# Multi-query attention on one core: fp16 transposes, fewer borrowed score buffers, and a new order of scores and weighted sums

## Chip, cores, metric

One NeuronCore of a Trainium2 chip. The metric is the device time of one execution in microseconds (us). All durations below are in us unless marked ns.

## What the kernel must compute

```python
# q: (8, 1024, 16, 64) float32; k, v: (8, 1024, 64) float32, shared by the 16 heads of a batch
scores  = q @ k^T / sqrt(64)
weights = softmax(scores)            # over the keys
out     = weights @ v                # (8, 1024, 16, 64) float32
```

Of the kernel before, what the change touches and what calls it, by code (L numbers as in the profile page):

```python
# [16 lines left out]
def kernel(  # L17
# [19 lines left out]
    KPS = NKT // SPG  # L37
    NP = (B * H) // 2
    HP = H // 2
    HHALF = H // 2  # L40
    scale = 1.0 / math.sqrt(D)

    consts = ctx.enter_context(tc.tile_pool(name="consts", bufs=1))
    qnatp = ctx.enter_context(tc.tile_pool(name="qnatp", bufs=2))
    kvp = ctx.enter_context(tc.tile_pool(name="kvp", bufs=2))
    qtp = ctx.enter_context(tc.tile_pool(name="qtp", bufs=3))
    wtp = ctx.enter_context(tc.tile_pool(name="wtp", bufs=2 * NKT + 2))
    otsp = ctx.enter_context(tc.tile_pool(name="otsp", bufs=4))
    recp = ctx.enter_context(tc.tile_pool(name="recp", bufs=4))
    osbp = ctx.enter_context(tc.tile_pool(name="osbp", bufs=3))  # L50

    scp = ctx.enter_context(tc.tile_pool(name="scp", bufs=3, space=bass.MemoryType.PSUM))
# [1 line left out]

    ident = consts.tile([P, P], FP32)
    make_identity(nc, ident)

    k2t: dict = {}
    vpr: dict = {}
    qnat: dict = {}  # L60
    qt_tiles: dict = {}
    wt_tiles: dict = {}
    ot_psum: dict = {}
# [3 lines left out]
    def emit_batch_load(b):  # L67
        if b >= B or b in k2t:
            return
        knat = kvp.tile([P, NKT, D], FP32, tag="knat", name=f"knat{b}")  # L70
        vnat = kvp.tile([P, NKT, D], FP32, tag="vnat", name=f"vnat{b}")
        nc.sync.dma_start(out=knat, in_=k[b].rearrange("(c p) d -> p c d", p=P))
        nc.sync.dma_start(out=vnat, in_=v[b].rearrange("(c p) d -> p c d", p=P))  # L73
        slabs = []
        for half in range(2):
            qn = qnatp.tile(
                [P, NKT, HHALF * D], FP32, tag="qnat", name=f"qnat{b}_{half}"
            )
            nc.sync.dma_start(
                out=qn,  # L80
                in_=q[b, :, half * HHALF : (half + 1) * HHALF, :].rearrange(
                    "(c p) h d -> p c (h d)", p=P
                ),
            )
            slabs.append(qn)
        qnat[b] = slabs
        kk = kvp.tile([P, S], FP16, tag="k2t", name=f"k2t{b}")
        n_stage = max(1, S // QCH)
        per = S // n_stage
        for cs in range(n_stage):  # L90
            kps = scp.tile([P, 2, QCH], FP32, tag="sc", name=f"kps{b}_{cs}")
            for jj in range(per // P):
                src = knat[:, cs * (per // P) + jj, :]
                nc.tensor.matmul(  # L94
                    kps[0:64, 0, jj * P : (jj + 1) * P],
                    src,
                    ident,
                    start=True,
                    stop=True,
                    tile_position=(0, 0),  # L100
                )
                nc.tensor.matmul(  # L102
                    kps[64:128, 0, jj * P : (jj + 1) * P],
                    src,
                    ident,
                    start=True,
                    stop=True,
                    tile_position=(0, 64),
                )
            nc.vector.tensor_copy(  # L110
                out=kk[:, cs * per : (cs + 1) * per], in_=kps[:, 0, 0:per]
            )
        k2t[b] = kk
        vp = kvp.tile([P, NKT, 66], FP16, tag="vpr", name=f"vpr{b}")
        nc.vector.tensor_copy(out=vp[:, :, 0:64], in_=vnat)  # L115
        nc.vector.memset(vp[:, :, 64:65], 1.0)
        vpr[b] = vp

    def emit_qtrans(p, part):
        if p >= NP:  # L120
            return
        b, hp = divmod(p, HP)
        emit_batch_load(b)
        if p not in qt_tiles:
            qt_tiles[p] = qtp.tile([P, S], FP16, tag="qt", name=f"qt{p}")
        qt = qt_tiles[p]
        nchunk = NQB // 2
        st = scp.tile([P, 2, QCH], FP32, tag="sc", name=f"qst{p}_{part}")
        half, hloc = divmod(2 * hp, HHALF)
        for c in range(nchunk):  # L130
            sc_idx = part * nchunk + c
            src = qnat[b][half][:, sc_idx, hloc * D : (hloc + 2) * D]
            nc.tensor.matmul(  # L133
                st[:, c // 4, (c % 4) * P : (c % 4) * P + P],
                src,
                ident,
                start=True,
                stop=True,
            )
        width = nchunk * P  # L140
        assert width <= QCH
        nc.vector.tensor_copy(  # L142
            out=qt[:, part * width : (part + 1) * width], in_=st[:, 0, 0:width]
        )

    def emit_qk(p, j, c):
        b = p // HP
        sc = scp.tile([P, 2, QCH], FP32, tag="sc", name=f"sc{p}_{j}_{c}")
        kk = k2t[b]
        qt = qt_tiles[p]  # L150
        nc.tensor.matmul(  # L151
            sc[:, 0, :],
            kk[0:64, j * P : (j + 1) * P],
            qt[0:64, c * QCH : (c + 1) * QCH],
            start=True,
            stop=True,
            tile_position=(0, 0),
        )
        nc.tensor.matmul(  # L159
            sc[:, 1, :],  # L160
            kk[64:128, j * P : (j + 1) * P],
            qt[64:128, c * QCH : (c + 1) * QCH],
            start=True,
            stop=True,
            tile_position=(64, 0),
        )
        key = (p, j)
        if key not in wt_tiles:
            wt_tiles[key] = wtp.tile([P, 2, S], FP16, tag="wt", name=f"wt{p}_{j}")
        wt = wt_tiles[key]  # L170
        nc.scalar.activation(  # L171
            out=wt[:, :, c * QCH : (c + 1) * QCH], in_=sc, func=EXP, scale=scale
        )
# [28 lines left out]

    def emit_finish(p, hh):
        b, hp = divmod(p, HP)
        ots = ots_tiles.pop((p, hh))
        if p not in osb_tiles:
            osb_tiles[p] = osbp.tile([P, NQB, 2 * D], FP32, tag="osb", name=f"osb{p}")
        osb = osb_tiles[p]
        for gq in range((NQB + 3) // 4):
            nblk = min(4, NQB - gq * 4)  # L210
            tr = scp.tile([P, 2, QCH], FP32, tag="sc", name=f"tr{p}_{hh}_{gq}")
            for i in range(nblk):
                qb = gq * 4 + i
                nc.tensor.matmul(  # L214
                    tr[:, 0, i * P : i * P + 65],
                    ots[0:65, qb * P : (qb + 1) * P],
                    ident[0:65, 0:65],
                    is_transpose=True,
                    start=True,
                    stop=True,  # L220
                )
            trv = tr[:, 0, :].rearrange("p (blk x) -> p blk x", x=P)[:, 0:nblk, :]
            rec = recp.tile([P, 4], FP32, tag="rec", name=f"rec{p}_{hh}_{gq}")
            nc.vector.reciprocal(out=rec[:, 0:nblk], in_=trv[:, :, 64:65])  # L224
            nc.vector.tensor_tensor(  # L225
                out=osb[:, gq * 4 : gq * 4 + nblk, hh * D : (hh + 1) * D],
                in0=trv[:, :, 0:64],
                in1=rec[:, 0:nblk].unsqueeze(2).broadcast_to([P, nblk, D]),
                op=mybir.AluOpType.mult,
            )  # L230
        if hh == 1:
            nc.sync.dma_start(
                out=out[b, :, 2 * hp : 2 * hp + 2, :].rearrange(
                    "(qb p) h d -> p qb (h d)", p=P
                ),
                in_=osb_tiles.pop(p),
            )

    emit_batch_load(0)
    emit_qtrans(0, 0)  # L240
    emit_qtrans(0, 1)
    stepA = (NGRP - 1) * SPG
    for w in range(NP + 2):
        pQK = w
        pAV = w - 1
        for j in range(NKT):
            if j == 0 and (w - 2, 1) in ots_tiles:
                emit_finish(w - 2, 1)
            if 0 <= pAV < NP:
                g = j // SPG  # L250
                sub = j % SPG
                emit_av(pAV, g, list(range(sub * KPS, (sub + 1) * KPS)))
            if pQK < NP:
                for c in range(NQC):
                    emit_qk(pQK, j, c)
            if j == 2:
                emit_qtrans(pQK + 1, 0)
            elif j == 3:
                emit_qtrans(pQK + 1, 1)
            if j == 5 and (pQK + 2) < NP and (pQK + 2) % HP == 0:  # L260
                emit_batch_load((pQK + 2) // HP)
            if j == stepA and (pAV, 0) in ots_tiles:
                emit_finish(pAV, 0)


# [28 lines left out]
```

## The kernel before

It works on 64 head pairs (8 batches of 8 pairs). In one round `w` of the main loop the scores and exponentials of pair `w` are made beside the weighted sums ("AV") of pair `w-1`. A round has eight rows `j`, one for each block of 128 keys. A row makes two score tiles of 128 keys x (2 heads x 512 queries), each turned into weights by one exponential on ScalarE. An added column of ones in v gives the softmax denominator.

```python
scp = ctx.enter_context(tc.tile_pool(name="scp", bufs=3, space=PSUM))   # score buffers, 2 banks each
otp = ctx.enter_context(tc.tile_pool(name="otp", bufs=2, space=PSUM))   # AV accumulators
...
def emit_qtrans(p, part):            # half of a q transpose: 4 blocks, fp32, one score buffer
    st = scp.tile([P, 2, QCH], FP32, tag="sc")
    for c in range(4):
        nc.tensor.matmul(st[:, 0, c*P:(c+1)*P], qnat_block_fp32, ident_fp32, start=True, stop=True)
    nc.vector.tensor_copy(out=qt[:, half], in_=st[:, 0, :])             # to fp16
...
def emit_finish(p, hh):              # output of one head: 2 x 4 transposes, two score buffers
    for gq in range(2):
        tr = scp.tile([P, 2, QCH], FP32, tag="sc")
        # 4 transposes of 65x128, then reciprocal and multiply on VectorE
...
for w in range(NP + 2):              # pQK = w, pAV = w - 1
    for j in range(8):
        if j == 0: emit_finish(w - 2, 1)
        emit_av(pAV, group j // 2, four key blocks)   # 4 matmuls of 512 columns
        emit_qk(pQK, j, 0); emit_qk(pQK, j, 1)        # scores, then exponential
        if j == 2: emit_qtrans(pQK + 1, 0)
        elif j == 3: emit_qtrans(pQK + 1, 1)
        if j == 5 and a new batch is near: emit_batch_load(...)   # loads; k transposes, fp32
        if j == 6: emit_finish(pAV, 0)
```

(Shortened: the real lines carry shapes and tile positions.) q, k and output transposes have no PSUM of their own. They borrow from the three score buffers through which scores flow to ScalarE.

The softmax here doesn't subtract the row's maximum and nothing guards it: scores larger than these inputs give would overflow.

## Time and profile before

| | before |
|---|---|
| time, median (range) of the first 4 runs | 1140.0 (1139.38 to 1140.86) |
| ScalarE busy (1024 exponentials: 965.6) | 966.9 of 1138.5 |
| ScalarE idle in front of exponentials | 158.2, of it 14.5 before the first |
| first exponential starts / last ends | 16.5 / 1125.9 |

A line of a timeline starts with the start and the duration; `x6` means that six equal instructions were merged into it, and the bracket at the end gives the engine's idle time just before and what ended it. A line of groups gives busy time and the mean ns of one, then the idle time ahead of the group and its main releaser.

### The profile page before, as it was taken

The numbers are of one execution on the slowest core, as the hardware profiler recorded it, in microseconds if no ns is written. First come the engines' busy times: TensorE is split into PE (matmuls) and PEld (weight loads), VectorE is DVE, ScalarE is ACT, GpSimd is POOL, SyncE is SP. The second block draws the span as 40 slices with busy tenths as digits, with TensorE's granted clock in tenths as the row PEclk, the third lists the DMA queues.
The fourth block names the chain that finished last, engine by engine and source line by source line (L and its number), as shares of the span: only waits on it lengthen the run. The fifth ranks groups of instructions, "written<-read, shape, count | busy, mean of one in ns | idle before, by whom it ended". The sixth has DMA issues, their size and how long they took to land.

```text
span 1138.5 us, 15747 instructions
## 1 busy us (share of the span) xinstructions
PE 1046.2 (92%) x6400; PEld 471.5 (41%) x6400; DVE 426.9 (37%) x928; ACT 966.9 (85%) x1025; POOL 0.7 (0%) x6
## 2 busy tenths in 40 slices
PE   6999999999999999999999999999999999999997
PEld 3434434434344344344443444444444434444443
DVE  1333343433333334333433334343343333433333
ACT  4988888888888888888888888888888888888885
POOL 0000000000000000000000000000000000000000
PEclk9999999999999999999999999999999999999999
DMA  7120312103121131211313013130220312101101
GB/s 212 30 100 19 121 40 79 59 20 120 47 93 38 38 103 47 97 33 39 102 47 112 19 39 106 33 111 19 70 80 19 112 37 89 42 19 37 37 20 55
DMA packets 99911, 72.30 MB, mean 64 GB/s; under 512 B 17920, under 2 KB 83456, under 8 KB 99840
## 3 DMA queue, kind: packets, MB, share of 16 engines
q1 hardware_dynamic: 99840, 71.31, 19.5%
q8 instruction: 50, 0.82, 0.3%
q14 instruction: 21, 0.17, 0.1%
HBM read 37.75 MB, written 33.55 MB: 63 GB/s over the span
## 4 chain that ended last, share of the span: by engine, by line
PE 49%; ACT 44%; issue 6%; DMA 1%; DVE 0%; ACTq 0%; SPq 0%
ACT wt L171 44%; PE ot L185 18%; PE qst L133 13%; PE sc L151 9%; PE tr L214 7%; PE kps L94 1%; DMA qnat<-in_q_dram 1%; PE sc L159 0%; ACTq L171 0%; DVE osb L225 0%; DVE ots L198 0%; PE kps L102 0%; DVE qt L142 0%; DVE rec L224 0%; SPq L73 0%
## 5 line engine op out<-in xcount | busy, mean ns | idle before, releaser
L171 ACT ACTIVATE wt<-sc 128x1024 f16<-128x1024 f32 x1024 | 965.6, 1038 | 158.2 <-PE sc L159 158.2
L185 PE MATMUL ot<-wt,vpr 128*65 128x512 f16 x2048 | 555.1, 383 | 0.2 <-DVE ots L198 0.2
L151 PE MATMUL sc<-qt,k2t 64*128 64x512 f16 x1024 | 326.0, 381 | 3.4 <-ACT wt L171 2.2
L159 PE MATMUL sc<-qt,k2t 64*128 64x512 f16 x1024 | 328.2, 382 | 0.0
L185 PEld LDWEIGHTS <-vpr 128*65 128x65 f16 x2048 | 195.1, 112 | 179.6 <-issue 100.2
L198 DVE COPY ots<-ot 65x512 f32<-65x512 f32 x256 | 175.2, 685 | 214.7 <-PE ot L185 214.7
L142 DVE CAST qt<-qst 128x512 f16<-128x512 f32 x128 | 88.5, 691 | 268.5 <-PE qst L133 268.5
L133 PE MATMUL qst<-ident,qnat 128*128 128x128 f32 x1024 | 149.6, 290 | 36.4 <-ACT wt L171 31.6
L133 PEld LDWEIGHTS qst<-ident,qnat 128*128 128x128 f32 x1024 | 125.4, 193 | 82.0 <-ACT wt L171 50.6
L214 PE MATMUL tr<-ident,ots 65*128 65x65 f32 x1024 | 118.5, 238 | 40.9 <-ACT wt L171 30.7
L151 PEld LDWEIGHTS <-k2t 64*128 64x128 f16 x1024 | 57.4, 94 | 210.0 <-issue 158.4
L214 PEld LDWEIGHTS tr<-ident,ots 65*128 65x128 f32 x1024 | 83.8, 142 | 143.7 <-ACT wt L171 117.3
L224 DVE RECIPROCAL rec<-tr 128x4 f32<-128x4 f32 x256 | 46.6, 182 | 198.3 <-PE tr L214 191.0
L225 DVE TENSOR_TENSOR osb<-tr,rec 128x256 f32<-128x256 f32 x256 | 108.6, 424 | 8.6
L159 PEld LDWEIGHTS <-k2t 64*128 64x128 f16 x1024 | 78.7, 93 | 36.5 <-issue 36.4
L94 PE MATMUL kps<-ident,knat 128*64 128x128 f32 x128 | 17.7, 296 | 6.5 <-DMA knat<-in_k_dram 4.0
L94 PEld LDWEIGHTS kps<-ident,knat 128*64 128x64 f32 x128 | 15.1, 148 | 10.2 <-ACT wt L171 5.7
L102 PE MATMUL kps<-ident,knat 128*64 128x128 f32 x128 | 17.7, 297 | 0.0
L110 DVE CAST k2t<-kps 128x512 f16<-128x512 f32 x16 | 11.1, 691 | 12.0 <-PE kps L102 12.0
L102 PEld LDWEIGHTS kps<-ident,knat 128*64 128x64 f32 x128 | 15.1, 148 | 0.0
L115 DVE CAST vpr<-vnat 128x512 f16<-128x512 f32 x8 | 3.3, 416 | 4.4 <-DMA vnat<-in_v_dram 4.4
L171 ACT ACT_TABLE_LOAD x1 | 1.3, 1283 | 0.7 <-PEq L278 0.7
(7 smaller groups left out, 1.4 us busy)
## 6 DMA issues: line engine op xcount, KB each, us to landing
qnat<-in_q_dram SPq DMA_DIRECT2D x16, 2048.0 KB, 7.9
out_dram<-osb SPq DMA_DIRECT2D x64, 512.0 KB, 3.2
knat<-in_k_dram SPq DMA_DIRECT2D x8, 256.0 KB, 4.1
vnat<-in_v_dram SPq DMA_DIRECT2D x8, 256.0 KB, 3.3
```

Of the source, the lines that this page charges most:

```text
L94: nc.tensor.matmul(kps[0:64, 0, jj * P : (jj + 1) * P], src, ident, start=True, stop=True, tile_position=(0, 0),)
L102: nc.tensor.matmul(kps[64:128, 0, jj * P : (jj + 1) * P], src, ident, start=True, stop=True, tile_position=(0, 64),)
L133: nc.tensor.matmul(st[:, c // 4, (c % 4) * P : (c % 4) * P + P], src, ident, start=True, stop=True,)
L142: nc.vector.tensor_copy(out=qt[:, part * width : (part + 1) * width], in_=st[:, 0, 0:width])
L151: nc.tensor.matmul(sc[:, 0, :], kk[0:64, j * P : (j + 1) * P], qt[0:64, c * QCH : (c + 1) * QCH], start=True, stop=True, tile_position=(0, 0),
L159: nc.tensor.matmul(sc[:, 1, :], kk[64:128, j * P : (j + 1) * P], qt[64:128, c * QCH : (c + 1) * QCH], start=True, stop=True, tile_position ...
L171: nc.scalar.activation(out=wt[:, :, c * QCH : (c + 1) * QCH], in_=sc, func=EXP, scale=scale)
L185: nc.tensor.matmul(ot[0:65, :], vp[:, j, 0:65], wt[:, hh, cq * QCH : (cq + 1) * QCH], start=(j == 0), stop=(j == NKT - 1),)
L198: nc.vector.tensor_copy(out=ots_tiles[tkey][0:65, cq * QCH : (cq + 1) * QCH], in_=ot[0:65, :])
L214: nc.tensor.matmul(tr[:, 0, i * P : i * P + 65], ots[0:65, qb * P : (qb + 1) * P], ident[0:65, 0:65], is_transpose=True, start=True, stop= ...
L224: nc.vector.reciprocal(out=rec[:, 0:nblk], in_=trv[:, :, 64:65])
L225: nc.vector.tensor_tensor(out=osb[:, gq * 4 : gq * 4 + nblk, hh * D : (hh + 1) * D], in0=trv[:, :, 0:64], in1=rec[:, 0:nblk].unsqueeze(2). ...
```

## The change

Its intent: take fp32 passes off TensorE, borrow fewer score buffers, and put scores where they are not late. The core of the diff:

```diff
-    qnatp = ... bufs=2        # two 2 MB q slabs a batch, fp32
+    qnatp = ... bufs=3        # four 1 MB slabs a batch, fp32
+    qn16p = ... bufs=5        # their fp16 casts
-    wtp   = ... bufs=2 * NKT + 2
+    wtp   = ... bufs=2 * NKT + 1
+    ident16 = fp16 copy of ident
 # k: cast first, 16 transposes into one score buffer, one eviction (before: two buffers, two evictions)
+        nc.vector.tensor_copy(out=kn16, in_=knat)
-        for cs in range(n_stage):
-            kps = scp.tile([P, 2, QCH], FP32, tag="sc")
+        kps = scp.tile([P, 2, QCH], FP32, tag="sc")
 # q: eight fp16 transposes into one score buffer, one eviction of 1024 columns
-    def emit_qtrans(p, part):      # 4 blocks, fp32
+    def emit_qtrans(p):            # 8 blocks, fp16
+        src16 = get_q16(b, slab)   # load of the slab and its cast, once for two pairs
 # output: eight transposes into one score buffer, one reciprocal, one multiply
-        for gq in range((NQB + 3) // 4):
-            tr = scp.tile([P, 2, QCH], FP32, tag="sc")
+        tr = scp.tile([P, 2, QCH], FP32, tag="sc")
 # order of a row
-            if j == 0: emit_finish(w - 2, 1)
-            emit_av(four); emit_qk(0); emit_qk(1)
-            if j == 2: emit_qtrans(pQK + 1, 0)
-            elif j == 3: emit_qtrans(pQK + 1, 1)
-            if j == 6: emit_finish(pAV, 0)
+            emit_qk(0)
+            if j in (2, 4, 6): emit_av(first two)
+            emit_qk(1)
+            emit_av(the rest)
+            if j == 1: emit_finish(w - 2, 1)
+            elif j == 3: emit_qtrans(pQK + 1)
+            elif j == 5: emit_finish(pAV, 0)
+            if j == 4: get_q16 for pair pQK + 2
```

(Cut: the order of the AV groups, 0-2-1-3 in place of 0-1-2-3, so that head 0 is complete after row 3; and eight reciprocal tiles in place of four.)

More of the change, by code (lines that the diff above doesn't have):

```diff
@@ L39 @@
     HP = H // 2
-    HHALF = H // 2
+    NSL = 4 if H >= 8 else 1
+    HSL = H // NSL
     scale = 1.0 / math.sqrt(D)
     consts = ctx.enter_context(tc.tile_pool(name="consts", bufs=1))
-    qnatp = ctx.enter_context(tc.tile_pool(name="qnatp", bufs=2))
+    qnatp = ctx.enter_context(tc.tile_pool(name="qnatp", bufs=3))
+    qn16p = ctx.enter_context(tc.tile_pool(name="qn16p", bufs=5))
     kvp = ctx.enter_context(tc.tile_pool(name="kvp", bufs=2))
     qtp = ctx.enter_context(tc.tile_pool(name="qtp", bufs=3))
-    wtp = ctx.enter_context(tc.tile_pool(name="wtp", bufs=2 * NKT + 2))
+    wtp = ctx.enter_context(tc.tile_pool(name="wtp", bufs=2 * NKT + 1))
     otsp = ctx.enter_context(tc.tile_pool(name="otsp", bufs=4))
-    recp = ctx.enter_context(tc.tile_pool(name="recp", bufs=4))
+    recp = ctx.enter_context(tc.tile_pool(name="recp", bufs=8))
     osbp = ctx.enter_context(tc.tile_pool(name="osbp", bufs=3))
@@ L56 @@
     make_identity(nc, ident)
+    ident16 = consts.tile([P, P], FP16)
+    nc.vector.tensor_copy(out=ident16, in_=ident)
     k2t: dict = {}
     vpr: dict = {}
-    qnat: dict = {}
+    qn16: dict = {}
     qt_tiles: dict = {}
@@ L70, in emit_batch_load @@
         knat = kvp.tile([P, NKT, D], FP32, tag="knat", name=f"knat{b}")
+        nc.sync.dma_start(out=knat, in_=k[b].rearrange("(c p) d -> p c d", p=P))
+        qn16[b] = {}
         vnat = kvp.tile([P, NKT, D], FP32, tag="vnat", name=f"vnat{b}")
-        nc.sync.dma_start(out=knat, in_=k[b].rearrange("(c p) d -> p c d", p=P))
         nc.sync.dma_start(out=vnat, in_=v[b].rearrange("(c p) d -> p c d", p=P))
-        slabs = []
-        for half in range(2):
-            qn = qnatp.tile(
-                [P, NKT, HHALF * D], FP32, tag="qnat", name=f"qnat{b}_{half}"
-            )
-            nc.sync.dma_start(
-                out=qn,
-                in_=q[b, :, half * HHALF : (half + 1) * HHALF, :].rearrange(
-                    "(c p) h d -> p c (h d)", p=P
-                ),
-            )
-            slabs.append(qn)
-        qnat[b] = slabs
+        kn16 = kvp.tile([P, NKT, D], FP16, tag="kn16", name=f"kn16{b}")
+        nc.vector.tensor_copy(out=kn16, in_=knat)
         kk = kvp.tile([P, S], FP16, tag="k2t", name=f"k2t{b}")
@@ L89, in emit_batch_load @@
         per = S // n_stage
+        kps = scp.tile([P, 2, QCH], FP32, tag="sc", name=f"kps{b}")
         for cs in range(n_stage):
-            kps = scp.tile([P, 2, QCH], FP32, tag="sc", name=f"kps{b}_{cs}")
             for jj in range(per // P):
-                src = knat[:, cs * (per // P) + jj, :]
+                src = kn16[:, cs * (per // P) + jj, :]
                 nc.tensor.matmul(
-                    kps[0:64, 0, jj * P : (jj + 1) * P],
-                    src,
-                    ident,
-                    start=True,
-                    stop=True,
-                    tile_position=(0, 0),
+                    kps[0:64, cs, jj * P : (jj + 1) * P], src, ident16,
+                    start=True, stop=True, tile_position=(0, 0),
                 )
                 nc.tensor.matmul(
-                    kps[64:128, 0, jj * P : (jj + 1) * P],
-                    src,
-                    ident,
-                    start=True,
-                    stop=True,
-                    tile_position=(0, 64),
-                )
-            nc.vector.tensor_copy(
-                out=kk[:, cs * per : (cs + 1) * per], in_=kps[:, 0, 0:per]
-            )
+                    kps[64:128, cs, jj * P : (jj + 1) * P], src, ident16,
+                    start=True, stop=True, tile_position=(0, 64),
+                )
+        nc.vector.tensor_copy(out=kk, in_=kps.rearrange("p a x -> p (a x)"))
         k2t[b] = kk
@@ L117, in emit_batch_load, with get_q16 @@
         vpr[b] = vp
-    def emit_qtrans(p, part):
+    def get_q16(b, slab):
+        if slab in qn16[b]:
+            return qn16[b][slab]
+        qn = qnatp.tile([P, NKT, HSL * D], FP32, tag="qnat", name=f"qnat{b}_{slab}")
+        nc.sync.dma_start(
+            out=qn,
+            in_=q[b, :, slab * HSL : (slab + 1) * HSL, :].rearrange(
+                "(c p) h d -> p c (h d)", p=P
+            ),
+        )
+        q16 = qn16p.tile([P, NKT, HSL * D], FP16, tag="qn16", name=f"qn16{b}_{slab}")
+        nc.vector.tensor_copy(out=q16, in_=qn)
+        qn16[b][slab] = q16
+        return q16
+    def emit_qtrans(p):
         if p >= NP:
@@ L126, in emit_qtrans @@
         qt = qt_tiles[p]
-        nchunk = NQB // 2
-        st = scp.tile([P, 2, QCH], FP32, tag="sc", name=f"qst{p}_{part}")
-        half, hloc = divmod(2 * hp, HHALF)
+        nchunk = NQB
+        slab, hloc = divmod(2 * hp, HSL)
+        src16 = get_q16(b, slab)
+        st = scp.tile([P, 2, QCH], FP32, tag="sc", name=f"qst{p}")
         for c in range(nchunk):
-            sc_idx = part * nchunk + c
-            src = qnat[b][half][:, sc_idx, hloc * D : (hloc + 2) * D]
+            sc_idx = c
             nc.tensor.matmul(
                 st[:, c // 4, (c % 4) * P : (c % 4) * P + P],
-                src,
-                ident,
+                src16[:, sc_idx, hloc * D : (hloc + 2) * D],
+                ident16,
                 start=True,
@@ L139, in emit_qtrans @@
             )
-        width = nchunk * P
-        assert width <= QCH
+        assert nchunk * P == 2 * QCH
         nc.vector.tensor_copy(
-            out=qt[:, part * width : (part + 1) * width], in_=st[:, 0, 0:width]
+            out=qt, in_=st.rearrange("p a x -> p (a x)")
         )
@@ L204, in emit_finish @@
         b, hp = divmod(p, HP)
-        ots = ots_tiles.pop((p, hh))
+        ots = ots_tiles[(p, hh)]
         if p not in osb_tiles:
@@ L208, in emit_finish @@
         osb = osb_tiles[p]
-        for gq in range((NQB + 3) // 4):
-            nblk = min(4, NQB - gq * 4)
-            tr = scp.tile([P, 2, QCH], FP32, tag="sc", name=f"tr{p}_{hh}_{gq}")
-            for i in range(nblk):
-                qb = gq * 4 + i
-                nc.tensor.matmul(
-                    tr[:, 0, i * P : i * P + 65],
-                    ots[0:65, qb * P : (qb + 1) * P],
-                    ident[0:65, 0:65],
-                    is_transpose=True,
-                    start=True,
-                    stop=True,
-                )
-            trv = tr[:, 0, :].rearrange("p (blk x) -> p blk x", x=P)[:, 0:nblk, :]
-            rec = recp.tile([P, 4], FP32, tag="rec", name=f"rec{p}_{hh}_{gq}")
-            nc.vector.reciprocal(out=rec[:, 0:nblk], in_=trv[:, :, 64:65])
-            nc.vector.tensor_tensor(
-                out=osb[:, gq * 4 : gq * 4 + nblk, hh * D : (hh + 1) * D],
-                in0=trv[:, :, 0:64],
-                in1=rec[:, 0:nblk].unsqueeze(2).broadcast_to([P, nblk, D]),
-                op=mybir.AluOpType.mult,
-            )
@@ L231, in emit_finish @@
-        if hh == 1:
-            nc.sync.dma_start(
-                out=out[b, :, 2 * hp : 2 * hp + 2, :].rearrange(
-                    "(qb p) h d -> p qb (h d)", p=P
-                ),
-                in_=osb_tiles.pop(p),
-            )
+        nblk = NQB
+        assert NQB == 8
+        tr = scp.tile([P, 2, QCH], FP32, tag="sc", name=f"tr{p}_{hh}")
+        for i in range(nblk):
+            qb = i
+            nc.tensor.matmul(
+                tr[:, i // 4, (i % 4) * P : (i % 4) * P + 65],
+                ots[0:65, qb * P : (qb + 1) * P],
+                ident[0:65, 0:65],
+                is_transpose=True,
+                start=True,
+                stop=True,
+            )
@@ new lines, in emit_finish @@
+        trv = tr.rearrange("p a (blk x) -> p (a blk) x", x=P)
+        rec = recp.tile([P, 8], FP32, tag="rec", name=f"rec{p}_{hh}")
+        nc.vector.reciprocal(out=rec[:, 0:nblk], in_=trv[:, :, 64:65])
+        nc.vector.tensor_tensor(
+            out=osb[:, :, hh * D : (hh + 1) * D],
+            in0=trv[:, :, 0:64],
+            in1=rec[:, 0:nblk].unsqueeze(2).broadcast_to([P, nblk, D]),
+            op=mybir.AluOpType.mult,
+        )
+        if True:
+            del ots_tiles[(p, hh)]
+            if hh == 1:
+                nc.sync.dma_start(
+                    out=out[b, :, 2 * hp : 2 * hp + 2, :].rearrange(
+                        "(qb p) h d -> p qb (h d)", p=P
+                    ),
+                    in_=osb_tiles.pop(p),
+                )
@@ L239 @@
+    GORDER = [0, 2, 1, 3] if NQC == 2 else [0, 1]
+    NFB = (NQB + 3) // 4
     emit_batch_load(0)
-    emit_qtrans(0, 0)
-    emit_qtrans(0, 1)
-    stepA = (NGRP - 1) * SPG
+    emit_qtrans(0)
     for w in range(NP + 2):
@@ L246 @@
         for j in range(NKT):
-            if j == 0 and (w - 2, 1) in ots_tiles:
-                emit_finish(w - 2, 1)
-            if 0 <= pAV < NP:
-                g = j // SPG
-                sub = j % SPG
-                emit_av(pAV, g, list(range(sub * KPS, (sub + 1) * KPS)))
-            if pQK < NP:
-                for c in range(NQC):
-                    emit_qk(pQK, j, c)
-            if j == 2:
-                emit_qtrans(pQK + 1, 0)
-            elif j == 3:
-                emit_qtrans(pQK + 1, 1)
-            if j == 5 and (pQK + 2) < NP and (pQK + 2) % HP == 0:
+            if 0 <= pAV < NP:
+                g = GORDER[j // SPG]
+                js = list(range((j % SPG) * KPS, (j % SPG + 1) * KPS))
+            if pQK < NP:
+                emit_qk(pQK, j, 0)
+            if 0 <= pAV < NP and j in (2, 4, 6):
+                emit_av(pAV, g, js[: KPS // 2])
+                js = js[KPS // 2 :]
+            if pQK < NP:
+                emit_qk(pQK, j, 1)
+            if 0 <= pAV < NP:
+                emit_av(pAV, g, js)
+            if j == 1 and (w - 2, 1) in ots_tiles:
+                emit_finish(w - 2, 1)
+            elif j == 3:
+                emit_qtrans(pQK + 1)
+            elif j == 5 and (pAV, 0) in ots_tiles:
+                emit_finish(pAV, 0)
+            if j == 4 and (pQK + 2) < NP:
+                bb, hpp = divmod(pQK + 2, HP)
+                if bb in qn16:
+                    get_q16(bb, (2 * hpp) // HSL)
+            elif j == 5 and (pQK + 2) < NP and (pQK + 2) % HP == 0:
                 emit_batch_load((pQK + 2) // HP)
-            if j == stepA and (pAV, 0) in ots_tiles:
-                emit_finish(pAV, 0)
 _INS = ['q', 'k', 'v']
```

## The prediction

> **What bounds the kernel now.** I read the page's busy shares first, then its chain, its groups and the waits, and last the timelines of ScalarE and TensorE over one head pair. (Durations are in us unless marked.)
>
> ```profile
> PE 1046.2 (92%) x6400; PEld 471.5 (41%) x6400; DVE 426.9 (37%) x928; ACT 966.9 (85%) x1025; POOL 0.7 (0%) x6
> ...
> PE 49%; ACT 44%; issue 6%; DMA 1%; DVE 0%; ACTq 0%; SPq 0%
> ...
> L171 ACT ACTIVATE wt<-sc 128x1024 f16<-128x1024 f32 x1024 | 965.6, 1038 | 158.2 <-PE sc L159 158.2
> L185 PE MATMUL ot<-wt,vpr 128*65 128x512 f16 x2048 | 555.1, 383 | 0.2 <-DVE ots L198 0.2
> ...
> L142 DVE CAST qt<-qst 128x512 f16<-128x512 f32 x128 | 88.5, 691 | 268.5 <-PE qst L133 268.5
> L133 PE MATMUL qst<-ident,qnat 128*128 128x128 f32 x1024 | 149.6, 290 | 36.4 <-ACT wt L171 31.6
> ...
> L225 DVE TENSOR_TENSOR osb<-tr,rec 128x256 f32<-128x256 f32 x256 | 108.6, 424 | 8.6
> ...
> L115 DVE CAST vpr<-vnat 128x512 f16<-128x512 f32 x8 | 3.3, 416 | 4.4 <-DMA vnat<-in_v_dram 4.4
> ```
>
> Two engines are nearly full and the chain alternates between them, so neither alone is the bound: they hold each other up. The matmul busy share includes pipeline tails, so I don't take 92% as a limit. ScalarE must run 1024 exponentials; its whole idle time of 158.2 is put down to the score matmuls. The ScalarE timeline of a head pair shows when:
>
> ```profile
> 562.37 5.61 ACT L171 ACTIVATE wt<-sc 128x1024 f16<-128x1024 f32 x6 [0.55 <-PE sc L159]
> 568.44 1.94 ACT L171 ACTIVATE wt<-sc 128x1024 f16<-128x1024 f32 x2 [0.46 <-PE sc L159]
> 570.83 5.61 ACT L171 ACTIVATE wt<-sc 128x1024 f16<-128x1024 f32 x6 [0.46 <-PE sc L159]
> 577.10 1.94 ACT L171 ACTIVATE wt<-sc 128x1024 f16<-128x1024 f32 x2 [0.66 <-PE sc L159]
> 579.59 5.61 ACT L171 ACTIVATE wt<-sc 128x1024 f16<-128x1024 f32 x6 [0.55 <-PE sc L159]
> ```
>
> From 562.37 to 579.59 is one pair: 17.22, with four gaps. Undisturbed, six exponentials take 5.61 and the last is 1.04 long, so the pitch is (5.61-1.04)/5 = 0.915, and sixteen need 14.64. The other 2.58 are four gaps (2.13 idle, and 0.11 more at each because the overlap with the next exponential is lost). TensorE shows their cause:
>
> ```profile
> 538.47 1.16 PE L133 MATMUL qst<-ident,qnat 128*128 128x128 f32 x8 [0.53 <-ACT wt L171]
> 539.47 1.03 PE L185 MATMUL ot<-wt,vpr 128*65 128x512 f16 x4
> 540.42 0.39 PE L151 MATMUL sc<-qt,k2t 64*128 64x512 f16 x1
> ...
> 540.65 0.38 PE L151 MATMUL sc<-qt,k2t 64*128 64x512 f16 x1
> ...
> 540.96 1.16 PE L133 MATMUL qst<-ident,qnat 128*128 128x128 f32 x8
> 541.96 1.03 PE L185 MATMUL ot<-wt,vpr 128*65 128x512 f16 x4
> 542.91 0.39 PE L151 MATMUL sc<-qt,k2t 64*128 64x512 f16 x1
> ```
>
> The score pool has three buffers, and the q transposes (qst) and output transposes (tr) borrow one each. When half a q transpose takes the buffer that an exponential just gave back, ScalarE has two scores left, 2 x 0.915 = 1.83 of work. TensorE needs 1.00 for the four fp32 blocks, 0.95 for four weighted-sum matmuls (AV) standing ahead of the next scores, and 0.50 from score start to exponential start (540.42 to 540.92): 2.45. That is the gap of 0.6. The output transposes do the same by taking two buffers per row of the loop.
>
> **What the Trainium skill says.** "ScalarE: Activation LUTs", section "What ACT_TABLE_LOAD costs": an ACTIVATE with immediates takes 186 ns + 0.833 N, so 1039 ns at N=1024, and neighbours overlap by about 93 ns. The trace agrees on the duration (1038 ns), but overlaps 0.12, so I use 0.915. "TensorE: Matmul & The Clock Gate", section "Back-to-back issue gap": isolated gaps of N/2.4 + 2.5 ns, about 216 ns at 512 columns and 56 at 128, but 81 ns in a stream of load-and-multiply pairs of 128. Here AV matmuls follow each other every 0.22; no fp16 transpose is in this trace, so 0.06 to 0.08 is an estimate from that page. "VectorE: DVE Perf Modes", section "The perf-mode tier table": an fp32 copy within SBUF runs at 2x, one out of fp32 PSUM at 1x. The trace agrees: 512 elements cost 416 ns from SBUF and 691 from PSUM. "TensorEngine Tiling (Array Packing)", section "Key Properties": changing the tiling mode drains TensorE. Here a turn between the row-tiled scores and full-array work costs about 0.1 each way (score to AV 0.31 against 0.22 between scores; AV to score 0.99 for 4 x 0.22).
>
> **The change, part by part.**
> 1. q is cast to fp16 before the transpose. An fp32 block appears as two passes (1024 matmuls for 64 pairs x 8 blocks); a pair's q cost 2 x 1.00. In fp16: 8 x 0.06 to 0.07 + 0.1 for the turn = 0.60. Removed: 1.4 of TensorE a pair, about 90 in all. Added: 32 casts of 128x2048, 416 ns + 1536/(2 x 0.96) = 1.22 each, 39 of VectorE, which is 63% idle.
> 2. Both halves of a q transpose share one score buffer; both quarters of an output transpose as well. Borrowed buffers fall from six a pair to three. TensorE time of the output transposes stays: four took 0.30 before the next instruction (549.89 to 550.19), eight in a row 8 x 0.077 + turn = 0.70, twice a pair. Eviction of q becomes 691 + 512/0.96 = 1224 ns instead of 2 x 691; the multiply 424 + 256/0.96 = 691 instead of 2 x 424.
> 3. Scores go ahead of AV, and in rows 2, 4 and 6 the AV matmuls are split 2 + 2 around the second score. This adds two turns in each of three rows, 0.2 a row, but never leaves more than 2 AV matmuls ahead of a score there.
> 4. k: fp16, one buffer, 8 concurrent block pairs x 0.06 + 0.1 = 0.6 instead of 2.0 (545.40 to 547.34), once a batch.
> 5. Loads of q: 1 MB slabs. One buffer less for weights (17), which still lets a tile be refilled only after its AV is three rows past.
>
> **TensorE demand of a pair, afterwards**, by rows of the loop: rows 0 and 7: 0.22+0.31+0.99 = 1.52 each; rows 1 and 5 (output transpose after AV): 0.22+0.31+0.87+0.70 = 2.10 each; row 3 (q): 0.22+0.31+0.87+0.60 = 2.00; rows 2, 4, 6: 2 x (0.31+0.55) = 1.72 each. Sum 14.40, against ScalarE's 14.64. So ScalarE becomes the bound, by only 0.24.
>
> **Does every score come in time?** Put the exponentials at 0, 0.915, ...; number n ends at 0.915n + 1.04 and frees its buffer 0.05 later; score n must start by 0.915n - 0.50. Walking TensorE through the rows with three buffers in turn, the tight places are these. Row 1: score 3 can start at 1.09, AV to 2.27, output transpose to 2.97; score 4 starts 2.97, limit 3.16. Row 3: AV to 6.10, q transpose to 6.70; score 8 starts 6.70, limit 6.82. Row 5: score 11 at 8.64, AV to 9.82, output transpose to 10.52; score 12 limit 10.48: late by 0.04. Everything after is early again, and buffers whose VectorE eviction must end come back in time (q at 8.0, needed at 8.4). So gaps shrink from 2.58 a pair to about 0.04, but with margins of 0.1 to 0.2. I allow 0.15 for them: 63 x 0.15 = 9.5.
>
> **Start, end, batch changes.** First exponential now at 16.54. A 1 MB slab should land at about 8.5 (an estimate: 2 MB took 7.9 alone and 10.7 here behind others), then cast 1.2, transposes at cold clock 0.9, eviction 1.2, score 0.5: 12.4. End: from the last exponential at 1125.9 to 1138.5 it is 12.6; AV is unchanged, the last transposes run eight together: 12.8. Seven batch changes: the k transposes borrow a fourth buffer; score 12 then waits for exponential 11, 11.16 against 10.48: 0.7 each, 5 in all (now a gap of 1.64 each).
>
> Sum: 12.4 + 1024 x 0.915 (937) + 9.5 + 5 + 12.8 = 977. I settle on 975.
>
> **Rivals.**
> A. TensorE becomes the bound. For: the demand differs by 0.24 a pair, and the fp16 blocks and turns are estimates. If an fp16 block costs 0.11 as an fp32 pass does, or each turn 0.05 more, the pair takes 15.0 to 15.4: 1000 to 1020. Against: rows without transposes in today's trace leave TensorE waiting for ScalarE.
> B. A q slab is loaded where its first transpose stands, in the first row of a new batch: issue, landing (about 5), cast 1.2, against about 3.7 of other work: 3 to 4 lost seven times, about +25, so 1000. Against: the load queue in this trace doesn't follow the program; it loads k for the next batch but one at 547.45, as soon as the buffer is free. With three slabs and five fp16 copies loads should be a batch ahead.
> C. VectorE blocks: a 1.22 cast ahead of an eviction holds a score buffer; every second pair loses up to 0.9, 30 in all: 1005. For: it works in order. Against: 6.6 busy of 14.6.
> D. Nothing gained because the output transposes, unchanged in fp32, cause two of the four gaps: half of 2.58 would stay, 1055. Against: a row then took two buffers, now one.
>
> **Range and chances.** The floor, with no gap at all, is 12 + 937 + 12 = 961, a few less if the start is quicker. A or B alone lead to about 1000. Range 957 to 1003. Faster by over 2% (below 1117): 0.97; within 2%: 0.02; slower: 0.01.
>
> **What would show it.** Right: ScalarE busy above 95% with runs far longer than six in its timeline; its idle time below 35 in place of 158; q transposes in eight fp16 matmuls within 0.6; the chain almost all ScalarE. Wrong by A: ScalarE idle in every pair with TensorE never waiting for it. By B: seven gaps of 3 or more, ended by a cast behind a q load. By C: gaps every second pair, with the cast just ahead of an eviction. By D: gaps that start at each output transpose.

## The result, and the profile after

| | before | after |
|---|---|---|
| time, median (range), runs | 1140.28 (1139.38 to 1140.98), 13 | 972.52 (971.81 to 973.62), 8 |
| TensorE / ScalarE / VectorE busy | 1046.2 / 966.9 / 426.9 | 943.7 / 941.3 / 404.0 |
| ScalarE idle ahead of exponentials (of it before the first) | 158.2 (14.5) | 16.8 (12.4) |
| a head pair, amid a batch | 17.22 | 14.67 (16 x 0.917) |

The ratio after to before is 0.853 (95% interval 0.852 to 0.854). Here and below a ratio compares fast runs of both kernels, as the record gives it; it isn't quite the ratio of the medians quoted.

The page after: busy shares, the chain of work that ended last, and the groups that answer to those shown of before.

```profile
PE 943.7 (97%) x5760; PEld 388.4 (40%) x5760; DVE 404.0 (42%) x641; ACT 941.3 (97%) x1025; POOL 0.7 (0%) x6
...
ACT 73%; PE 16%; issue 9%; DMA 1%; DVE 1%; SPq 0%; ACTq 0%
...
L169 ACT ACTIVATE wt<-sc 128x1024 f16<-128x1024 f32 x1024 | 940.0, 1159 | 16.8 <-PE sc L157 16.8
...
L132 PE MATMUL qst<-ident,qn 128*128 128x128 f16 x512 | 39.9, 222 | 4.5 <-DVE qn L114 4.5
L114 DVE CAST qn<-qnat 128x2048 f16<-128x2048 f32 x32 | 38.9, 1215 | 9.9 <-DMA qnat<-in_q_dram 9.9
```

The chain moves to ScalarE (44% to 73%), and the idle time ahead of the exponentials falls from 158.2 to 16.8. Both engines now show 97%. That does not say which one binds; a run below does. The q transposes are 512 matmuls in place of 1024 fp32 passes.

The ScalarE timeline after, from the start:

```profile
14.38 7.44 ACT L169 ACTIVATE wt<-sc 128x1024 f16<-128x1024 f32 x8 [12.36 <-PE sc L157]
22.49 91.77 ACT L169 ACTIVATE wt<-sc 128x1024 f16<-128x1024 f32 x100 [0.68 <-PE sc L157]
114.80 117.54 ACT L169 ACTIVATE wt<-sc 128x1024 f16<-128x1024 f32 x128 [0.54 <-PE sc L157]
```

Before, no run was longer than six from the steady state to the last pair, with four gaps a pair. Now a run is a whole batch of 128, and the only gaps are one at the start (0.68) and one at each of the seven changes of batch (0.54). The whole time is then accounted for: 14.4 to the first exponential, 940.0 of exponentials, 0.68 + 7 x 0.54 = 4.5 of gaps, and 13.0 from the last exponential to the end. The pitch of undisturbed exponentials, from end to end, follows from the runs of 128 that take 117.44: a lone exponential lasts 1.02, and (117.44 - 1.02) / 127 = 0.917. It is the same in the trace before and in seven others. All 1024 at this pitch would take 938.8; of the 940.0 the rest is overlap lost at the gaps.

The TensorE timeline after, around a q transpose and an output transpose (of each score pair only the first half is shown):

```profile
536.51 1.05 PE L183 MATMUL ot<-wt,vpr 128*65 128x512 f16 x4
537.40 0.61 PE L132 MATMUL qst<-ident,qn 128*128 128x128 f16 x8
...
537.94 0.39 PE L149 MATMUL sc<-qt,k2t 64*128 64x512 f16 x1
...
541.12 0.66 PE L212 MATMUL tr<-ident,ots 65*128 65x65 f32 x8
...
541.70 0.39 PE L149 MATMUL sc<-qt,k2t 64*128 64x512 f16 x1
```

From the start of a q transpose to the next score it is 0.54, for all eight blocks; before, four blocks cost 1.00 and four AV matmuls stood between them and the score. An output transpose of eight costs 0.58.

### The profile page after: what moved, and what is told of

It is laid out like the page before. It is cut to its first block, busy times and chain, and to the rows that moved or that the text cites. A ratio compares the mean times of both kernels' runs of the same rounds, so it can differ in the third digit from the quotient of the medians.

```text
span 971.9 us, 14008 instructions
## 1 busy us (share of the span) xinstructions
PE 943.7 (97%) x5760; PEld 388.4 (40%) x5760; DVE 404.0 (42%) x641; ACT 941.3 (97%) x1025; POOL 0.7 (0%) x6
## 4 chain that ended last, share of the span: by engine, by line
ACT 73%; PE 16%; issue 9%; DMA 1%; DVE 1%; SPq 0%; ACTq 0%
ACT wt L169 73%; PE ot L183 8%; PE sc L149 6%; PE tr L212 2%; DMA qnat<-in_q_dram 1%; PE sc L157 0%; PE qst L132 0%; DVE qt L140 0%; DVE qn L114 0%; DVE k2t L96 0%; DVE ots L196 0%; DVE osb L223 0%; SPq L78 0%; SPq L75 0%; DVE rec L222 0%
## 5 line engine op out<-in xcount | busy, mean ns | idle before, releaser
L169 ACT ACTIVATE wt<-sc 128x1024 f16<-128x1024 f32 x1024 | 940.0, 1159 | 16.8 <-PE sc L157 16.8
L149 PE MATMUL sc<-qt,k2t 64*128 64x512 f16 x1024 | 352.4, 383 | 12.2 <-ACT wt L169 2.2
L157 PE MATMUL sc<-qt,k2t 64*128 64x512 f16 x1024 | 355.6, 386 | 0.0
L183 PEld LDWEIGHTS <-vpr 128*65 128x65 f16 x2048 | 171.9, 111 | 261.3 <-issue 195.4
L223 DVE TENSOR_TENSOR osb<-tr,rec 128x512 f32<-128x512 f32 x128 | 88.5, 691 | 4.4
L212 PE MATMUL tr<-ident,ots 65*128 65x65 f32 x1024 | 84.6, 225 | 0.6 <-DVE ots L196 0.5
L140 DVE CAST qt<-qst 128x1024 f16<-128x1024 f32 x64 | 77.5, 1210 | 4.3 <-PE qst L132 4.3
L132 PE MATMUL qst<-ident,qn 128*128 128x128 f16 x512 | 39.9, 222 | 4.5 <-DVE qn L114 4.5
L114 DVE CAST qn<-qnat 128x2048 f16<-128x2048 f32 x32 | 38.9, 1215 | 9.9 <-DMA qnat<-in_q_dram 9.9
L132 PEld LDWEIGHTS <-qn 128*128 128x128 f16 x512 | 34.6, 99 | 19.0 <-DVE qn L114 4.7
L222 DVE RECIPROCAL rec<-tr 128x8 f32<-128x8 f32 x128 | 24.9, 194 | 3.6 <-PE tr L212 3.6
L96 DVE CAST k2t<-kps 128x1024 f16<-128x1024 f32 x8 | 9.7, 1215 | 0.0
```

The costliest lines, as they stand in the source:

```text
L96: nc.vector.tensor_copy(out=kk, in_=kps.rearrange("p a x -> p (a x)"))
L114: nc.vector.tensor_copy(out=q16, in_=qn)
L132: nc.tensor.matmul(st[:, c // 4, (c % 4) * P : (c % 4) * P + P], src16[:, sc_idx, hloc * D : (hloc + 2) * D], ident16, start=True, stop=True,)
L140: nc.vector.tensor_copy(out=qt, in_=st.rearrange("p a x -> p (a x)"))
L149: nc.tensor.matmul(sc[:, 0, :], kk[0:64, j * P : (j + 1) * P], qt[0:64, c * QCH : (c + 1) * QCH], start=True, stop=True, tile_position=(0, 0),
L157: nc.tensor.matmul(sc[:, 1, :], kk[64:128, j * P : (j + 1) * P], qt[64:128, c * QCH : (c + 1) * QCH], start=True, stop=True, tile_position ...
```

## The experiments

The change has three parts. **F**: fp16 for q and k, with its slabs and casts. **M**: merged buffers, so that a q, output or k transpose borrows one score buffer in place of two. **O**: the new order of the loop. The first runs take all eight combinations of the three; the two corners are the kernels before and after. Each part's edit is its share of the diff above, for instance

```diff
 # M undone (F and O kept): halves and quarters with their own buffers
-        tr = scp.tile(...)                 # eight transposes
+        for gq in range(2):
+            tr = scp.tile(...)             # four transposes
-            elif j == 3: emit_qtrans(pQK + 1)
+            elif j == 2: emit_qtrans(pQK + 1, 0)
+            elif j == 3: emit_qtrans(pQK + 1, 1)
 # F undone (M and O kept): transposes from the fp32 slabs, two 2 MB slabs a batch, no casts,
 #   18 weight buffers as before
 # O undone (F and M kept): the row order of the kernel before
```

| parts in | median | ratio to before (95%) |
|---|---|---|
| none (before) | 1140.3 | 1 |
| F | 1041.7 | 0.914 (0.913 to 0.916) |
| M | 1125.3 | 0.988 (0.986 to 0.989) |
| O | 1124.1 | 0.987 (0.985 to 0.988) |
| F M | 1023.3 | 0.898 (0.897 to 0.900) |
| F O | 1064.7 | 0.935 (0.933 to 0.936) |
| M O | 1062.8 | 0.933 (0.932 to 0.934) |
| F M O (after) | 972.5 | 0.853 (0.852 to 0.854) |

The rows were timed each against the kernel before on the same chip. (Medians are of fast runs. F bundles the number format with the smaller slabs, the casts and one weight buffer less; these were not separated.) The theory throughout is that of the prediction: when a transpose borrows a score buffer, ScalarE lives on the scores that are left, and a gap appears where TensorE's work up to the next finished score is longer than that.

**F alone.**

> The kernel before with fp16 alone: q and k are cast first and transposed as fp16, loads and casts as in the change; each half still borrows its own score buffer, and the order of the loop is the old one. Theory (a gap appears where TensorE's work between a borrowed buffer and the next score exceeds the 1.83 us that ScalarE still has): half a q transpose falls from 1.00 to about 0.36, so 0.36 + 0.95 + 0.50 = 1.81, just under 1.83: the two q gaps (0.7 each with the lost overlap) vanish, the two gaps at the output transposes (0.57 each) stay. About 17.22 - 1.4 = 15.8 a pair, 1040 us. Rival (TensorE's summed work is the bound; nothing but its saving counts): the demand falls below ScalarE's, so this alone brings it to about 975 us.

1041.7, two above the theory's number and far from the rival's 975. The profiled execution (1395.7 at a granted clock of 0.561, the share of TensorE's full clock that it got) is left out, and its trace is not used. So the kernel was profiled once more:

> The kernel with fp16 alone once more, for a profile in the fast state, as the first one fell at a clock of 0.56. Theory: two gaps a pair of 0.46 idle, both directly behind output transposes, none behind q transposes; 1041 to 1043 us. Rival: gaps of about half the old size behind all four.

1041.3, a single run of unknown state that agrees with the fast ones. Its ScalarE timeline:

```profile
503.85 12.94 ACT L172 ACTIVATE wt<-sc 128x1024 f16<-128x1024 f32 x14 [0.46 <-PE sc L160]
517.24 1.94 ACT L172 ACTIVATE wt<-sc 128x1024 f16<-128x1024 f32 x2 [0.46 <-PE sc L160]
519.64 12.94 ACT L172 ACTIVATE wt<-sc 128x1024 f16<-128x1024 f32 x14 [0.46 <-PE sc L160]
```

Two gaps of 0.46 a pair remain, the size of those that output transposes made before; the two larger ones behind the q transposes (0.67 and 0.55) are gone. A pair takes 15.79.

**M alone.**

> The kernel before with merged score buffers alone (fp32 transposes, old order): a q transpose or an output transpose borrows one buffer in place of two. Theory: q in one piece needs 2.0 + 0.95 + 0.50 = 3.45 against 1.83, one gap of 1.6 in place of two of 0.6; output transposes 0.70 + 0.95 + 0.50 = 2.15 against 1.83, gaps of 0.3 in place of 0.46. The two effects cancel: 1130 to 1150 us, no gain. Rival (the borrowed buffers as such are what costs): gaps halve, about 1060 us.

1125.3: a gain of 1.2%, a little more than the cancelling that I expected, and nowhere near the rival. Its timeline over one pair:

```profile
509.45 1.94 ACT L164 ACTIVATE wt<-sc 128x1024 f16<-128x1024 f32 x2 [0.23 <-PE sc L152]
511.60 7.44 ACT L164 ACTIVATE wt<-sc 128x1024 f16<-128x1024 f32 x8 [0.21 <-PE sc L152]
520.60 5.60 ACT L164 ACTIVATE wt<-sc 128x1024 f16<-128x1024 f32 x6 [1.56 <-PE sc L152]
```

The large gap is 1.56, where the arithmetic had said 1.6; the small ones are 0.23 and 0.21 in place of 0.3.

**O alone.**

> The kernel before with the new order alone (scores ahead of AV, AV split in rows 2, 4, 6, output transposes after AV in rows 1 and 5; fp32, halves with own buffers). Theory: TensorE's demand of a pair is 3 x 1.72 + 5 x 1.51 + 2.1 for q + 1.5 for the output transposes = 16.3, above ScalarE's 14.64, so TensorE binds: some 16.3 to 16.6 a pair, 1065 to 1090 us. Rival (only summed TensorE work counts, and the order adds turns): no faster than before, 1140 to 1160 us.

1124.1: the theory's number was missed by 34 to 59. Its ScalarE timeline over one pair:

```profile
505.54 7.44 ACT L167 ACTIVATE wt<-sc 128x1024 f16<-128x1024 f32 x8 [0.54 <-PE sc L155]
513.52 1.94 ACT L167 ACTIVATE wt<-sc 128x1024 f16<-128x1024 f32 x2 [0.54 <-PE sc L155]
515.73 1.94 ACT L167 ACTIVATE wt<-sc 128x1024 f16<-128x1024 f32 x2 [0.27 <-PE sc L155]
518.20 3.77 ACT L167 ACTIVATE wt<-sc 128x1024 f16<-128x1024 f32 x4 [0.53 <-PE sc L155]
522.51 7.44 ACT L167 ACTIVATE wt<-sc 128x1024 f16<-128x1024 f32 x8 [0.54 <-PE sc L155]
```

A pair takes 16.97 (505.54 to 522.51), with the same four gaps, now 0.54, 0.27, 0.53 and 0.54. I had computed TensorE's summed demand, 16.3, and taken that as the period. But TensorE waits for free score buffers, also in rows without a transpose: the second score at 510.28 starts 0.53 after the first, and 0.22 is the distance where nothing is waited for. Four such late starts in this pair make about 1.0. With three buffers it cannot work ahead for the rows that need more. Gaps are decided borrowing by borrowing, not by the sum over a pair.

**F and M, old order.**

> The changed kernel with the old order of the loop put back (fp16 and merged buffers stay). Theory: q transpose 0.60 + 0.95 + 0.50 = 2.05 against 1.83, a gap of 0.22 + 0.11; two output transposes 2.15 against 1.83, 0.32 + 0.11 each: 1.2 a pair more than ScalarE's 14.68, about 1045 us. Rival (summed TensorE work alone): demand is lower than in the changed kernel by the turns, 14.1, so it is as fast or faster: 965 to 973 us.

1023.3, which is 51 slower than with the new order, although the new order adds turns between tiling modes (from row-tiled scores to matmuls on the full array and back). So the rival falls. The theory's 1045 was too high; its ScalarE timeline shows by how much:

```profile
525.38 13.15 ACT L169 ACTIVATE wt<-sc 128x1024 f16<-128x1024 f32 x14 [0.21 <-PE sc L157]
538.76 1.94 ACT L169 ACTIVATE wt<-sc 128x1024 f16<-128x1024 f32 x2 [0.23 <-PE sc L157]
540.92 13.15 ACT L169 ACTIVATE wt<-sc 128x1024 f16<-128x1024 f32 x14 [0.21 <-PE sc L157]
```

Output transposes leave gaps of 0.23 and 0.21, not 0.32, because eight cost 0.55 to 0.58 and not 0.70. The q transpose, at 0.44 before the AV that follows it, leaves no gap in this view. It isn't free: the run of 14 around it takes 13.15, against 12.94 in F alone, so 0.21 is lost inside the run. With it a pair adds up to 15.54.

**F and O, buffers split.**

> The changed kernel with the borrowed buffers split again: each half of a q transpose, each quarter of an output transpose and each half of the k transposes takes its own score buffer; fp16 and the new order stay. Theory (gaps come from how long ScalarE lasts on the scores left after a borrowing; slack of other rows can't be carried over): output transposes take two buffers at once and leave one score, so 0.54 idle + 0.11 twice a pair as in the run of the order alone; q halves in fp16 cost nothing. 14.68 + 1.3 = 16.0 a pair, about 1050 us, slower than fp16 alone in the old order. Rival (the three parts add up: fp16 -97, order -15, merging -14 us): about 1027 us.

1064.7. The direction of the theory holds: the new order without merged buffers is slower by 23 than no new order at all, so the parts don't add up. The size was 15 short: the gaps are 0.68 and not 0.54, twice a pair. In this trace three AV matmuls stand between the second quarter of an output transpose and the next score, two in the trace of F alone. I had not foreseen that; how much of the 0.14 it explains was not tried.

**M and O, fp32.**

> The changed kernel with fp32 transposes put back (straight from 2 MB slabs, no casts); merged buffers and new order stay. Theory: q in one piece takes 2.0 + 0.3 + 0.50 = 2.8 against the 1.78 that two scores last, one gap of about 1.0 + 0.11 a pair, none at the output transposes: 15.7 to 15.8 a pair, 1035 to 1045 us. Rival (the parts add up): 1140 - 15 - 14 = about 1110 us.

1062.8: far from the rival's 1110, and 18 to 28 above the theory. The gap amid a batch was right, one a pair, behind the q transpose:

```profile
525.81 14.87 ACT L164 ACTIVATE wt<-sc 128x1024 f16<-128x1024 f32 x16 [1.06 <-PE sc L152]
541.73 14.87 ACT L164 ACTIVATE wt<-sc 128x1024 f16<-128x1024 f32 x16 [1.06 <-PE sc L152]
```

That is 15.92 a pair, against 15.7 to 15.8 expected. I had left out the fp32 k transposes: at the change of batch in this trace one gap more, of 1.89, stands behind them. 64 x 0.17 and 7 x 2.0 make 25, about what the theory is short of.

**Is there slack in TensorE's sum, or only behind the borrowing?** Here each q transpose of the changed kernel is done twice into the same place.

```diff
-        for c in range(nchunk):
+        for c in [c for _ in range(2) for c in range(nchunk)]:
```

> The changed kernel with every fp16 q transpose done twice into the same place (result unchanged): 8 x 0.06 = 0.47 more of TensorE a pair. Summed demand is then about 14.7, equal to ScalarE's. Theory (only the time behind the borrowed buffer counts, margin there 0.1 to 0.3): a gap of 0.2 to 0.4 a pair, 985 to 998 us. Rival (sums count, and TensorE's waits elsewhere in the pair, some 0.5, swallow it): 972 to 977 us.

994.7 (ratio 0.873), within the theory's 985 to 998; the rival's 972 to 977 falls. The transposes now take 0.99 (533.11 to 534.10) before the next score, 0.45 more, and the pair 15.03, 0.36 more, with an idle gap in each pair behind the q transpose:

```profile
519.56 14.87 ACT L169 ACTIVATE wt<-sc 128x1024 f16<-128x1024 f32 x16 [0.17 <-PE sc L157]
534.59 14.86 ACT L169 ACTIVATE wt<-sc 128x1024 f16<-128x1024 f32 x16 [0.17 <-PE sc L157]
```

So of 0.45 only about 0.1 was free. Read one by one, the exponential behind the q transpose ends 0.27 late (0.17 idle and 0.10 of lost overlap), the one behind the next output transpose another 0.10. So the margin behind the q transpose was 0.45 - 0.27 = 0.18. The prediction's walk had 0.12 there with a q transpose of 0.60; with the 0.54 measured it is 0.18.

**Which of the two engines at 97% binds?** Here half of the AV matmuls are left out.

```diff
         for j in jlist:
+            if j % 2:
+                continue
...
-                stop=(j == NKT - 1),
+                stop=(j == NKT - 2),
```

> The changed kernel with the weighted sums over odd key blocks left out (result wrong on purpose): 16 of 32 AV matmuls a pair, 3.5 us of TensorE, are gone. Theory (ScalarE binds; 1024 exponentials at 0.918): only the seven batch gaps (0.65 each) and the tail (some 3 us) shrink, 964 to 970 us. Rival (TensorE at 97% busy is the bound): 64 x 3.5 less, about 750 us.

970.1 (967.7 to 973.1). Its output is wrong, which doesn't matter for the time. Taking away 3.5 of TensorE work in each pair, some 220 in all, moves the time by about 2. ScalarE is the bound, and TensorE's 97% is not a limit. The two groups in its trace:

```profile
L169 ACT ACTIVATE wt<-sc 128x1024 f16<-128x1024 f32 x1024 | 940.3, 1275 | 16.1 <-PE sc L157 15.9
L185 PE MATMUL ot<-wt,vpr 128*65 128x512 f16 x1024 | 356.3, 398 | 2.3 <-DVE ots L198 1.9
```

From the first exponential to the end of the last it is 944.9 here and 944.5 in the changed kernel; what the profiled run gained lies before and after them. (The granted clock was 0.975 to 0.988 in these runs, so the range is wider than elsewhere.)

**Towards a faster version.** Two edits aim at what is left besides exponentials, the start and the changes of batch.

```diff
-    qnatp = ctx.enter_context(tc.tile_pool(name="qnatp", bufs=3))
+    qnatp = ctx.enter_context(tc.tile_pool(name="qnatp", bufs=1))      # one_slab, both
-            elif j == 5 and (pQK + 2) < NP and (pQK + 2) % HP == 0:
+            elif j == 7 and (pQK + 2) < NP and (pQK + 2) % HP == 0:    # k_row7, both
```

> The changed kernel with one fp32 q slab buffer in place of three, so that at the start the first slab is loaded without two others beside it, and later each slab is loaded only after the cast of the one before. Theory (first exponential waits for the first slab, which landed at 10.1 us beside the others; a slab alone takes 5.2 us to land; after the start loads have two head pairs, 29 us, to land): first exponential at about 11.8 in place of 14.4, no new gaps, 969.5 to 971 us. Rival (three buffers are needed to hide the loads): new gaps every second pair, over 980 us.

972.3, so no gain was measured. The rival falls all the same: with a single slab buffer no gap was added, and two of the three slabs can be given up. The first exponential came at 13.6 in place of 14.4, not 11.8. The chain at the start of the changed kernel shows what else lies there:

```profile
1.84 8.23 DMA qnat<-in_q_dram
10.08 0.02 issue
10.10 1.23 DVE qn L114
11.33 1.13 DVE k2t L96
12.46 1.23 DVE qt L140
```

The q slab still took 7.5 to land with no other q slab in flight (7.46 in that run's chain, against 8.23 here and 6.78 in the next run); the k and v loads of the next batch were issued right behind it, and whether they slow it was not tried. The eviction of k, ready since about 7, waits behind the cast of q and stands in the chain with 1.13, but it costs little: the q transposes run beside it, from 11.38 to 12.41, and the eviction of q could not have started before they ended. This start also varies: the next run has the same start as the changed kernel, and its first exponential came at 12.9. So 13.6 against 14.4 shows nothing.

> The changed kernel with the next batch's k transposes put behind row 7 in place of row 5, so that they don't borrow a score buffer directly behind an output transpose. Theory: the seven gaps of 0.54 (0.65 with lost overlap) at the batch changes shrink to 0.0 to 0.3, so 2.5 to 4.5 us less, 968 to 970 us. Rival (the batch gap is the time of the k transposes themselves and goes where they go): 972 to 973 us.

970.6 (ratio 0.852). The seven gaps are gone from its timeline:

```profile
20.73 934.94 ACT L169 ACTIVATE wt<-sc 128x1024 f16<-128x1024 f32 x1016 [0.36 <-PE sc L157]
```

Yet these 1016 exponentials take 934.9 from first to last, and in the changed kernel the same number takes 936.4, gaps included. So of 3.8 of idle time only 1.4 was saved. Read one by one, undisturbed exponentials keep the pitch of 0.917 in both traces, but at each change of batch five of them here end 0.03 to 0.18 late, 0.44 in all, in place of one that ends 0.65 late. Most of that is lost overlap, which the merged timeline doesn't show as a gap: an unbroken run is not yet an undisturbed engine. So the truth lies between theory and rival.

> Both of these edits together. Theory: they touch different times, so the savings add: 965.5 to 968.5 us, with exponentials in unbroken runs from the first head pairs to the end. Rival (k lands late without the early loads, or the edits collide at a batch change): no better than the better of the two.

971.0 (ratio 0.852, 95% interval 0.851 to 0.853). All 1024 exponentials form one unbroken run of 942.3 (938.8 at the pitch of 0.917), but the time is no better than with the second edit alone, and the interval overlaps that of the changed kernel. Neither edit is shown to beat it.

## Why the prediction came out as it did

The predicted 975 lies 0.3% from the measured 972.5, but some of its terms were wrong in opposite directions, so the closeness of the number is in part luck.

| term | predicted | measured in the trace after |
|---|---|---|
| start to the first exponential | 12.4 | 14.4 |
| 1024 exponentials | 937 | 940.0 |
| gaps amid the batches | 9.5 (allowance) | 0, after one of 0.68 at the start |
| seven batch changes | 5 | 3.8 |
| last exponential to the end | 12.8 | 13.0 |

- **Mechanism: right.** The borrowed buffer and the work up to the next finished score decide the gaps. F alone, with its two remaining gaps of 0.46, and the doubled q transposes are the clearest evidence. Of the signs named beforehand, ScalarE's busy share (97%), the long runs, the idle time (16.8) and the eight q transposes within 0.6 came true; the chain is 73% ScalarE and not almost all.
- **Part 1 (fp16).** The step is right; 0.60 was a bit high, it is 0.54. From the doubled run an fp16 block costs 0.45 / 8 = 56 ns. The cast of a slab was put at 1.22 with a rate of 2 x 0.96 columns per ns, for which the prediction names no source; the trace after has 418 ns for 512 columns and 1215 ns for 2048, which is 1.93 columns per ns and agrees.
- **Part 2 (merging).** The count of buffers was right; an output transpose costs 0.58 and not 0.70. These two over-estimates made the margins look smaller than they were and led to the allowance of 9.5, which nothing in the trace needed. The allowance hid errors at the start (2.0) and in the exponentials (3.0).
- **Part 3 (order).** That it pays in spite of its extra turns is shown by taking it away (972.5 to 1023.3). What the prediction did not say, and the eight combinations show, is how much this hangs on merged buffers: with them the order gains 51 in fp16 and 63 in fp32 (1125.3 to 1062.8); without them it gains 16 in fp32 and loses 23 in fp16.
- **Part 4 (k).** 0.6 was right: 349.64 to 350.21 in the trace after.
- **Demand of a pair, 14.40 against 14.64.** Which engine binds was right, as the halved AV shows. The comparison of sums as such is weak: it was the step that failed for O alone.
- **Pitch.** 0.915 was a reading slightly too low: a lone exponential lasts 1.02 and not the mean of 1.04, so a run of six gives (5.61 - 1.02) / 5 = 0.918, and the long runs 0.917. That is some 2 of the 3.0.
- **Start.** The slab landed at 10.1 and not 8.5; the q transposes took 1.03 and not 0.9, and the first score 0.65 and not 0.5. (The terms written down add to 12.3.)
- **Rivals.** A (TensorE) falls by the halved AV. Its 15.0 to 15.4 a pair doesn't follow from its own figures: a block at 0.11 adds 8 x 0.05 to 14.40, which is 14.8, and 0.05 on each of 22 turns makes 15.5. B (a late slab) falls: VectorE waited for q loads five times, 9.9 in all, all before 28; with one slab buffer no gap was added either. C (VectorE) falls: no gaps every second pair. D falls: no gaps behind output transposes, but for the seven places where k transposes follow one.

## What to carry to other kernels

When short jobs borrow from the buffers that feed the bound engine, ask of each borrowing how long that engine lasts on what is left and how long the next item takes to appear; a sum of busy time over the whole period doesn't answer that. Shorten the job, borrow once instead of twice, and put the next item ahead of other work: here the three parts gave 8.6%, 1.2% and 1.3% alone, 14.7% together, and the new order without merged buffers cost 23 in fp16. Two engines at 97% busy are told apart by taking work away from one of them.

## What the Trainium skill lacked or had wrong

- "ScalarE: Activation LUTs", section "What ACT_TABLE_LOAD costs": neighbours overlap by about 93 ns there, which makes 946 ns at 1024 elements. Here the pitch was 0.917 in runs of any length, which is 122 ns less than the 1039 ns of the page's formula.
- "TensorE: Matmul & The Clock Gate", section "Back-to-back issue gap": of its two figures at 128 columns, 56 ns isolated and 81 ns in a stream of load-and-multiply pairs, the first fits here: eight more fp16 transposes, each with its own weights, cost 0.45, so 56 ns each.
- No page gives a time for an fp32 block of 128 columns. Here four took 1.00 in the trace before and eight 1.89 in M alone, so one more costs 0.22, four times an fp16 block.
- "TensorEngine Tiling (Array Packing)", section "Key Properties", says that changing the mode drains TensorE, without a figure. Here a turn cost about 0.1 each way.
- "Perfetto Trace Analysis", in its opening note, calls matmul busy time a bad metric for the distance to the limit. The runs agree: at 97% busy, leaving out half of the AV matmuls changed the time by about 2.
